# Seven half-products for each pair of second-layer blocks, layer norms by chunk, stepped keys and values, another order of the last blocks

## The chip, the core and the metric

The kernel runs on one core of one Trainium2 chip. The metric is device time in microseconds, the median over runs: 1499.7 us for the kernel before (three runs, 1498.29 to 1500.64). In the text PE is the matrix engine, DVE the vector engine, ACT the scalar engine, POOL the GpSimd engine, and SP the engine from whose queue most DMAs start.

## What is computed

A backbone of two layers over 1024 latent tokens and 256 context tokens of width 1024. Each layer is

```python
h = modulate(rms_norm(x), shift, scale)          # context tokens: a learned constant conditioning
p = h @ w_in                                     # one projection, columns split in head groups
# A: 2-D neighbourhood attention (4 heads of 64, window 8 x 16, plus all context keys)
# B: latent attention: rank-256 queries, rank-128 keys and values, 2-D rotary key
# C: gelu(u) * (layer_norm(v) mixed over 128-token chunks by a 128x128 matrix, 4 groups of 64)
# D: gated depthwise convolution, 3 taps over the tokens
y = concat(A, B, C, D) * silu(gates)
x = x + gate * (y @ w_out)
```

and the output is an RMS norm of the latent tokens. The second layer's context tokens feed nothing after their keys and values.

## The kernel before

Values that enter a matmul are held as two rounded parts, hi and lo, whose sum is the fp32 value. A product of two such values is three matmuls per 128-row slice of the contraction: hi times hi, hi times lo, lo times hi (the helper at L159; transposes go through L162). The normalised input H lies in SBUF with features on the partitions and is cut in token chunks: 0 and 1 of 512 latent tokens each, 2 of 256 context tokens.

`layer(l)` runs in stages. Group C's `cu` and `cv` come first: `cv_tokens` makes the 256 columns of v for 128 tokens at a time, takes mean and variance in 4 groups and normalises the tile (DVE, with a power on POOL in `rstd_of`, L204 to L209, between), and `cv_gate` mixes the normalised tokens by small matmuls. Then `proj` runs over blocks of 128 output columns: cg, dc, dh, db, dg, the value tiles of A (`wav`, 10 tiles of 128 tokens by 288 columns), ckv, cq, ak, aq, bg and ag, two blocks of each but ckv. One block is a 512 KB weight DMA, a cast to hi on ACT (L346), a subtraction for lo on POOL (L351), and for every chunk 24 matmuls (8 slices of the contraction, 3 each) of 512 columns into one PSUM bank, which ACT, DVE or POOL reads off.

Latent attention runs in 8 units of 256 queries (`Mla`). `mla_load` fetches the stored parts, `mla_keys` makes one head pair's keys (evacuated by L770 and L771), `mla_values` all values (L788). Neighbourhood attention follows in 16 units (`Na`); `scores_to` lets the score matmuls run ahead of the rest. `merged` multiplies the heads' results by the gates and splits them (L1134, L1135). `out_block(fb)` then makes 128 columns of the output projection and adds the residual, and `finish` normalises a chunk for the next layer or for the output. In both layers chunk 0's out blocks are put between the last attention units, and the blocks for the other chunks follow after the attention.

SBUF space is a set of tags with so many buffers each (g 24, x 20, wh, wl, wr and st 2 each), and PSUM has 5 banks of the large kind (`psb`). The order of the instructions on each engine is set by a scheduler from the order of the code, data and buffers, except between `pe.chain(True)` and `pe.chain(False)`, where PE keeps the written order. All engines run their queues in order.

## Time and profile before

| | |
|---|---|
| median of 3 runs | 1499.7 us (1498.29 to 1500.64) |
| profiled execution | 1495.95 us, span of its instructions 1494.2 us |
| mean granted clock of PE | 0.992 |
| PE busy | 1422.2 us, 95% of the span |
| weight loads of PE | 1195.2 us, 80% (beside the matmuls) |
| DVE busy | 765.6 us, 51% |
| ACT busy | 573.8 us, 38% |
| POOL busy | 459.2 us, 31% |
| chain that ended last | PE 80%, issue 5%, DVE 5%, POOL 5%, ACT 3%, DMA 1% |

The busy times are sums over the whole span. The chain is the work that ended last, followed back to what released each step, so its shares say which engine would have to be faster for an earlier end. The second layer starts at about 839 us with the first `cu` matmul, its attention at about 1153 us, and the blocks after the attention at about 1426 us.

### The profile page before, as it was taken

Reading aid. Unit: us, or ns where it says so; the run is one execution under the profiler, and the core shown is the slowest. Engines: PE = TensorE matmul, PEld = TensorE weight load, DVE = VectorE, ACT = ScalarE, POOL = GpSimd, SP = SyncE. Lnnn points to the kernel's source line nnn. Section 1 sums busy time; section 2 is a strip of 40 time slices with the busy share of each in tenths; the row PEclk is TensorE's granted clock in tenths of the full one; section 3 lists DMA queues with packets and bytes.
Section 4 is the critical chain, followed back from the end, with each engine's and each line's share of the span. In section 5 each row is a group of like instructions: output and inputs, shape, how many; then the busy total and the mean of one; then the engine's idle time right before and its main releaser. Section 6 shows DMA issues by size and latency. Waiting matters only on the chain.

```text
span 1494.2 us, 23065 instructions
## 1 busy us (share of the span) xinstructions
PE 1422.2 (95%) x8964; PEld 1195.2 (80%) x8964; DVE 765.6 (51%) x1873; ACT 573.8 (38%) x1303; POOL 459.2 (31%) x369
## 2 busy tenths in 40 slices
PE   4999999999998999999999999999999899989987
PEld 2788888988886777678878978898888777778877
DVE  5968657063027666664464752201212677755474
ACT  5611111122227565563342421112223666655542
POOL 2145343041230001536522253412332000155741
PEclk9999999999999999999999999999999999999999
DMA  9513324355451004946333101123465012375331
GB/s 354 191 46 113 106 94 171 103 184 179 142 118 24 1 22 116 166 124 174 124 117 127 37 28 44 46 78 127 163 221 115 0 36 43 104 179 156 100 127 57
DMA packets 80943, 166.46 MB, mean 111 GB/s; under 512 B 8129, under 2 KB 34753, under 8 KB 80705
## 3 DMA queue, kind: packets, MB, share of 16 engines
q1 hardware_dynamic: 63808, 136.66, 27.6%
q0 software_dynamic: 15936, 27.27, 9.0%
q8 instruction: 70, 1.15, 0.3%
q10 hardware_dynamic: 1088, 1.05, 0.2%
q14 instruction: 41, 0.33, 0.1%
HBM read 135.33 MB, written 33.82 MB: 113 GB/s over the span
## 4 chain that ended last, share of the span: by engine, by line
PE 80%; issue 5%; DVE 5%; POOL 5%; ACT 3%; DMA 1%; DVEq 0%; SPq 0%; POOLq 0%; ACTq 0%
PE psb L159 65%; PE pst L162 7%; PE psv L159 7%; PE pst L159 1%; POOL g L1135 1%; POOL s L204 1%; POOL wh L348 1%; POOL wl L351 1%; DVE s L206 1%; DVE s L835 1%; DVE g L494 1%; ACT g L982 1%; ACT pt L731 1%; DMA wr<-in_wtb 1%; DVE pt L729 0%
## 5 line engine op out<-in xcount | busy, mean ns | idle before, releaser
L159 PE MATMUL psb<-g,wh 128*128 128x512 f32 (+1 forms) x2400 | 686.9, 372 | 2.6 <-ACT g L1134 1.5
L159 PEld LDWEIGHTS psb<-g,wh 128*128 128x128 f32 x2400 | 431.7, 189 | 88.1 <-issue 2.0
L159 PE MATMUL psb<-g,wl 128*128 128x512 f32 (+1 forms) x1200 | 443.5, 370 | 2.0 <-DVE wl L351 1.2
L159 PEld LDWEIGHTS psb<-g,wl 128*128 128x128 f32 x1200 | 226.2, 189 | 44.4 <-DVE wl L351 1.6
L351 POOL TENSOR_TENSOR wl<-wr,wh 128x1024 fp32r<-128x1024 f32 (+2 forms) x64 | 150.2, 2348 | 304.9 <-ACT wh L346 297.6
L159 PE MATMUL psb<-g,st 128*128 128x512 f32 (+1 forms) x616 | 160.5, 380 | 11.7 <-DVE g L771 2.9
L835 DVE TENSOR_REDUCE s<-psb 128x1 f32<-128x512 f32 (+1 forms) x200 | 117.1, 589 | 87.7 <-PE psb L159 85.7
L159 PE MATMUL psb<-g,g 128*128 128x256 f32 (+2 forms) x832 | 135.6, 307 | 5.3 <-ACT g L346 3.1
L159 PEld LDWEIGHTS psb<-g,st 128*128 128x128 f32 x616 | 98.6, 193 | 35.6 <-issue 13.5
L159 PEld LDWEIGHTS psb<-g,g 128*128 128x128 f32 x832 | 112.3, 194 | 11.6 <-ACT g L346 3.3
L346 ACT CAST wh<-wr 128x1024 fp32r<-128x1024 f32 (+2 forms) x56 | 56.0, 1006 | 168.6 <-PE psb L159 139.6
L159 PE MATMUL psv<-pt,g 128*64 128x256 f32 (+1 forms) x1312 | 119.5, 331 | 0.6 <-ACT pt L731 0.5
L731 ACT COPY pt<-pst 128x512 f32<-128x512 f32 x116 | 67.9, 585 | 110.1 <-PE pst L162 108.7
L159 PEld LDWEIGHTS psv<-pt,g 128*64 128x64 f32 x1312 | 79.3, 137 | 32.1 <-issue 7.8
L326 DVE CUSTOM_DVE_ANT_0 tmp<-g,x 128x512 f32<-128x512 f32 x112 | 94.3, 893 | 8.2 <-POOL x L459 7.2
L162 PE MATMUL pst<-ident,g 128*128 128x128 f32 x464 | 81.3, 278 | 13.7 <-ACT g L982 7.5
L729 DVE COPY pt<-pst 128x512 f32<-128x512 f32 x116 | 79.0, 683 | 11.7 <-PE pst L162 10.8
L204 POOL TENSOR_TENSOR s<-s,mhalf 128x4 f32<-128x4 f32 (+3 forms) x35 | 37.1, 1060 | 155.0 <-DVE s L264 64.3
L1165 DVE SCALAR_TENSOR_TENSOR x<-psb,modG,x 128x512 f32<-128x512 f32 (+1 forms) x48 | 29.4, 615 | 100.9 <-PE psb L159 59.2
L162 PEld LDWEIGHTS pst<-ident,g 128*128 128x128 f32 x464 | 55.6, 140 | 30.8 <-ACT g L982 10.3
L348 POOL TENSOR_SCALAR wh<-wr 128x1024 fp32r<-128x1024 f32 x16 | 44.4, 2772 | 106.5 <-PE pst L162 64.9
L159 PE MATMUL psb<-st,g 128*128 128x288 f32 (+1 forms) x456 | 64.3, 289 | 0.0
(187 smaller groups left out, 1850.2 us busy)
## 6 DMA issues: line engine op xcount, KB each, us to landing
g<-in_wmod SPq DMA_DIRECT2D x48, 512.0 KB, 4.4
wr<-in_wtb SPq DMA_DIRECT2D x46, 512.0 KB, 3.5
wr<-in_wout SPq DMA_DIRECT2D x27, 512.0 KB, 3.7
st<-in_nab SPq DMA_DIRECT2D x24, 384.0 KB, 3.7
x<-in_xT SPq DMA_DIRECT2D x32, 256.0 KB, 5.6
g<-scr_q POOLq DMA_DIRECT2D x32, 256.0 KB, 7.0
x<-x SPq DMA_DIRECT2D x24, 256.0 KB, 2.4
g<-scr_k POOLq DMA_DIRECT2D x20, 256.0 KB, 5.4
```

Of the source, the lines that this page charges most:

```text
L159: return self._next(nc.tensor.matmul(*p, **k))
L162: return self._next(nc.tensor.transpose(*p, **k))
L204: pool.tensor_tensor(r0, v, mhalf[:, :n], ALU.pow)
L206: dve.scalar_tensor_tensor(t, v, -0.5, r0, ALU.mult, ALU.mult)
L326: dve.tensor_tensor_reduce(junk, w[:, hf * 512:hf * 512 + 512], crow[cond, hf], 1.0, 0.0, ALU.mult, ALU.add, part[:, i, cond, hf:hf + 1])
L346: act.copy(hi, raw)
L348: pool.tensor_scalar(hi, raw, 1.0, None, ALU.mult)
L351: (pool if lo_eng == "pool" else dve).tensor_tensor(lo, raw, f(hi), ALU.subtract)
L729: dve.tensor_copy(dst, src)
L731: act.copy(dst, src)
L835: dve.reduce_max(st["mx"][:, i:i + 1], s_, AX.X)
L1165: dve.scalar_tensor_tensor(xa, p, mod[l]["G"][:, fb, cond:cond + 1], xa, ALU.mult, ALU.add)
```

## The change

In the second layer, blocks 0 and 1 of a kind and chunks 0 and 1 form a two by two product, whose contraction is cut in halves as well. `proj2` computes it by 7 half-products (Winograd's form of Strassen's method), each of 12 matmuls of 512 columns, in place of 4 blocks-by-chunks of 24. Half-products are of sums of weight quarters and sums of quarters of H; two banks keep accumulating over several half-products, and their values in between are copied off (`m1`, `u2`, `z5`). The sums of H are made once, in `right_parts` and `right_sums`, and the sums of weights for every pair, with their own hi and lo. What only context tokens need (ak for chunk 2), ckv and the value tiles come first, in the written order of `paired`. 

In both layers the layer norm of group C takes one power for a chunk and two wide DVE operations, keys are allocated and their DMAs issued ahead (`keys_alloc`), values are made in five steps between the scores, and the second head pair's keys one chunk at a time among the pieces of unit 1. The last out blocks run in the order 7, 0 to 6; block 7 takes the weights that chunk 0's block 7 left, and the norm of chunk 0 ends later. Some of the buffers are in pools that share memory by phase.

```diff
         def cv_tokens(c):
             nt = CHUNKS[c][1] // 128
             vns[c] = T("g", [nt, 4, 64])
+            mv = T("s", [nt, 4, 2])
             for i in range(nt):
                 t = c * 4 + i
                 p = PS("b", [256])
                 mm3(p, [(htok(t, kc, 0), htok(t, kc, 1), wcv(kc, 0), wcv(kc, 1)) for kc in range(KC)])
-                gv = T("v1", [4, 64])
-                act.activation(gv, p.rearrange("p (g n) -> p g n", g=4), AF.Gelu)
+                act.activation(vns[c][:, i], p.rearrange("p (g n) -> p g n", g=4), AF.Gelu)
                 st6 = T("s", [4, 6])
-                mv = T("s", [4, 2])
                 for g in range(4):
-                    dve.bn_stats(st6[:, g, :], gv[:, g, :])
+                    dve.bn_stats(st6[:, g, :], vns[c][:, i, g, :])
                 for g in range(4):
-                    dve.bn_aggr(mv[:, g, :], st6[:, g, :])
-                ve = T("s", [4])
-                dve.tensor_scalar(ve, mv[:, :, 1], EPS, None, ALU.add)
-                r = rstd_of(ve, 4)
-                for g in range(4):
-                    dve.tensor_scalar(vns[c][:, i, g, :], gv[:, g, :], mv[:, g, 0:1], r[:, g:g + 1],
-                                      ALU.subtract, ALU.mult)
+                    dve.bn_aggr(mv[:, i, g, :], st6[:, g, :])
+            ve = T("s", [nt, 4])
+            dve.tensor_scalar(ve, mv[:, :, :, 1], EPS, None, ALU.add)
+            r = rstd_of(ve.rearrange("p t g -> p (t g)"), nt * 4)
+            vn = vns[c].rearrange("p t g n -> p (t g) n")
+            mean = mv.rearrange("p t g k -> p (t g) k")[:, :, 0:1]
+            dve.tensor_tensor(vn, vn, mean.to_broadcast([128, nt * 4, 64]), ALU.subtract)
+            dve.tensor_tensor(vn, vn, r.unsqueeze(2).to_broadcast([128, nt * 4, 64]), ALU.mult)
...
+        def w_op(raw, lo_eng="pool"):
+            t = T(("wh", "wl")[nop[0] % 2], [2, 512], F32R)
+            nop[0] += 1
+            split(t[:, 0, :], t[:, 1, :], raw, lo_eng=lo_eng)
+            return t.rearrange("p h (k n) -> p h k n", k=4)
...
+        def right_parts(i):
+            t = {}
+            for k, (c, kc) in enumerate(((0, i), (1, i), (1, i + 4), (0, i + 4))):
+                t[k] = T("x", [512])
+                pool.tensor_tensor(t[k], f(H[c, kc][:, 0, :]), f(H[c, kc][:, 1, :]), ALU.add)
+            R["11", i], R["21", i], R["22", i] = H[0, i], H[0, i + 4], H[1, i + 4]
+            return t
+        def right_sums(i, t):
+            for name, o, p_, q_ in (("1", 0, 1, 0), ("3", 1, 2, 1), ("2", 2, 2, 0), ("4", 3, 3, 2)):
+                after(dve.tensor_tensor(t[o], t[p_], t[q_], ALU.subtract), gated[1])
+                r = R[name, i] = T("o" if i > 1 and name in "34" else "g", [2, 512], F32R)
+                split(r[:, 0, :], r[:, 1, :], t[o], lo_eng="dve" if name in "12" else "pool")
+        def product(p, w, name, first=True):
+            n = 0
+            for i in range(4):
+                r = R[name, i]
+                for wl_, rl_ in ((0, 0), (0, 1), (1, 0)):
+                    pe.matmul(p, w[:, wl_, i, :], r[:, rl_, :], start=first and n == 0, stop=n == 11,
+                              skip_group_check=True)
+                    n += 1
+        def proj2(base, evac, mid=None):
+            r = {}
+            for j in range(2):
+                for k in range(2):
+                    r[j, k] = T("x", [512])
+                    sp.dma_start(r[j, k], a["wtb"][l, BLOCKS.index(f"{base}{j}")][:, k * 512:(k + 1) * 512])
+            q = T("wr", [2, 512])
+            a11, a12 = w_op(r[0, 0]), w_op(r[0, 1])
+            dve.tensor_tensor(q[:, 1, :], r[0, 0], r[1, 0], ALU.subtract)
+            dve.tensor_tensor(r[1, 0], r[1, 0], r[1, 1], ALU.add)
+            dve.tensor_tensor(q[:, 0, :], r[1, 0], r[0, 0], ALU.subtract)
+            dve.tensor_tensor(r[0, 1], r[0, 1], q[:, 0, :], ALU.subtract)
+            s2, s1 = w_op(q[:, 0, :], "dve"), w_op(r[1, 0])
+            x_, y_ = PS("b", [512]), PS("b", [512])
+            product(x_, a11, "11")
+            m1 = T("tmp", [512])
+            act.copy(m1, x_)
+            product(y_, a12, "21")
+            dve.tensor_tensor(m1, y_, m1, ALU.add)
+            evac(0, m1, 0)
+            s3 = w_op(q[:, 1, :], "dve")
+            product(x_, s2, "2", False)
+            u2 = T("tmp", [512])
+            act.copy(u2, x_)
+            s4 = w_op(r[0, 1], "dve")
+            z_ = PS("b", [512])
+            product(z_, s1, "1")
+            z5 = T("tmp", [512])
+            dve.tensor_copy(z5, z_)
+            if mid is not None:
+                mid()
+            a22 = w_op(r[1, 1])
+            product(x_, s3, "3", False)
+            dve.tensor_tensor(z5, x_, z5, ALU.add)
+            evac(1, z5, 1)
+            product(z_, s4, "22", False)
+            dve.tensor_tensor(u2, z_, u2, ALU.add)
+            evac(1, u2, 0)
+            product(x_, a22, "4", False)
+            evac(0, x_, 1)
...
+        def paired():
+            wav = w_tok(a["wav"][l], 288, ("o", "o"), ("o", "o"))
+            block_c("ak0", 2, lambda c, p: k_evac(c, p, 0))
...
+            w = w_block(a["wtb"][l, BLOCKS.index("ckv0")])
+            ckv_block(2, *w)
+            ckv_block(1, *w)
+            ckv_block(0, *w)
+            cv_gate(0)
+            parts = [right_parts(0)]
+            block_c("ak1", 2, lambda c, p: k_evac(c, p, 1))
+            for fns in late[1:]:
+                fns.pop(0)()
+            av_tile(8, wav)
+            late[-1].pop()()
+            parts.append(right_parts(1))
+            for t in (9, 4):
+                av_tile(t, wav)
+            cv_gate(1)
+            for i in range(2):
+                right_sums(i, parts[i])
+            for t in (5, 6, 7):
+                av_tile(t, wav)
+            for i in range(2, 4):
+                right_sums(i, right_parts(i))
+            for t in range(4):
+                av_tile(t, wav)
+            pe.chain(False)
+            av_windows()
+            proj2("cg", lambda c, p, j: gate(c, p, 4 + j))
...
+            proj2("dc", lambda c, p, j: act.copy(map_(6 + j, c), p))
+            proj2("dh", conv_in)
...
+            proj2("db", mulb)
+            proj2("dg", lambda c, p, j: gate(c, p, 6 + j))
+            proj2("cq", cq_evac)
+            proj2("ak", k_evac)
+            proj2("aq", lambda c, p, j: q_evac(c, p, j, 0.125))
+            cq_stats()
+            proj2("bg", lambda c, p, j: act.activation(map_(2 + j, c), p, AF.Silu))
...
+        def keys_alloc(pair):
+
             K = Ks[pair] = {}
             kctx = T("g", [2, 2, 256], F32R)
+            for c in (2, 0, 1):
+                o, n = CHUNKS[c]
+                for h in range(2):
+                    t = K[h, c] = T("g", [2, n], F32R) if c < 2 else kctx[:, h]
+                    pool.dma_start(t[64:128], scr["kr"][:, :, o:o + n].rearrange("h p n -> p h n"))
...
+                evac(vts[c][:, i:i + 2, :], p, "DA"[c == 1 and i == 0])
+            return [lambda c=c, i=i: step(c, i) for c in range(3) for i in range(0, CHUNKS[c][1] // 128, 2)]
...
+                (dve if c == 1 and fc < 2 else pool).tensor_tensor(t[:, 1, :], m, f(t[:, 0, :]), ALU.subtract)
+        tail = (7, 0, 1, 2, 3, 4, 5, 6)
...
+            proj2("ag", lambda c, p, j: act.activation(map_(j, c), p, AF.Silu), lambda: (mla_load(), mla_keys(0), units[0].prep()))
+            ph.close()
...
+            if u == 1:
+                for n, c in enumerate((2, 0, 1)):
+                    ps_.insert(3 * n + 2, lambda c=c: mla_keys(1, (c,)))
+                ps_.insert(0, lambda: keys_alloc(1))
...
-        scores_to(4)
-        mla_values()
-        scores_to(7)
-        mla_keys(1)
+        for k, fn in enumerate(mla_values()):
+            scores_to(3 + 2 * k)
+            fn()
...
             ks2 = [(1, 0, 512), (2, 0, 256)]
-            for fb in range(8):
-                out_block(fb, ks2, lo_eng="dve")
+            for fb in tail:
+                out_block(fb, ks2, kept[7] if fb == 7 else None, lo_eng="dve")
+                if fb == 7:
+                    rest = stats_sums(accs[k0], 512)
                 if fb == 0:
-                    finish(k0)
+                    finish(k0, rest)
...
             pe.chain(True)
             for i in range(2):
                 k = (1, 256 * i, 256)
-                for fb in range(8):
-                    if i == 0:
+                done = k0 if i == 0 else (1, 0, 256)
+                for fb in tail:
+                    if i == 0 and fb < 7:
                         split(*ws[fb], raws[fb], lo_eng="dve" if fb % 2 == 0 else "pool")
-                    out_block(fb, [k], [t.rearrange("p (k n) -> p k n", k=8) for t in ws[fb]])
-                    done = k0 if i == 0 else (1, 0, 256)
-                    if fb == 0:
+                    out_block(fb, [k], kept[7] if fb == 7 else [t.rearrange("p (k n) -> p k n", k=8) for t in ws[fb]])
+                    if fb == 7:
                         rest = stats_sums(accs[done], done[2], more.get(done))
-                    if fb == 2:
+                    if fb == 1:
                         finish(done, rest)
```

The order of PE's instructions changes as follows in three places. First the start of cg in the second layer; before, with the first chunk's first block (`psb_8893`) and the second chunk's (`psb_8921`), where `wh` and `wl` are the block's hi and lo:

```order
L159 MATMUL psb_8893<-g_7677,wh_8889 128x512 x2
L159 MATMUL psb_8893<-g_7677,wl_8890 128x512
L159 MATMUL psb_8893<-g_7682,wh_8889 128x512 x2
L159 MATMUL psb_8893<-g_7712,wh_8889 128x512 x2
L159 MATMUL psb_8893<-g_7712,wl_8890 128x512
L159 MATMUL psb_8921<-g_8237,wh_8889 128x512 x2
L159 MATMUL psb_8921<-g_8237,wl_8890 128x512
```

and now, one row of each of the products called 11 and 21 (`psb_9381`, `psb_9382`), then the whole products called 1 (`psb_9433`) and 2 (again `psb_9381`), and the first rows of product 3:

```order
L173 MATMUL psb_9381<-g_7639,wh_9365 128x512 x3
L173 MATMUL psb_9382<-g_7659,wl_9368 128x512 x3
L173 MATMUL psb_9433<-g_9070,wl_9378 128x512 x3
L173 MATMUL psb_9433<-g_9086,wl_9378 128x512 x3
L173 MATMUL psb_9433<-g_9197,wl_9378 128x512 x3
L173 MATMUL psb_9433<-g_9221,wl_9378 128x512
L173 MATMUL psb_9381<-g_9078,wh_9375 128x512 x3
L173 MATMUL psb_9381<-g_9094,wh_9375 128x512 x3
L173 MATMUL psb_9381<-g_9205,wh_9375 128x512 x3
L173 MATMUL psb_9381<-g_9229,wh_9375 128x512 x3
L173 MATMUL psb_9433<-g_9221,wl_9378 128x512 x2
L173 MATMUL psb_9381<-g_9074,wh_9413 128x512 x3
```

A bank is taken up again by a later product after its value has been copied off; the scheduler has put ten of the twelve matmuls of product 1 ahead of product 2, and two behind it.

Second the start of the second layer's latent attention; before, the keys of the first head pair (`psb_10731` and the two after it) among the blocks of ag:

```order
L159 MATMUL psb_10676<-g_7712,wh_10639 128x512 x2
L159 MATMUL psb_10676<-g_7712,wl_10640 128x512
L159 MATMUL psb_10703<-g_7677,wh_10645 128x512 x2
L159 MATMUL psb_10731<-g_10662,g_10659 128x256 x3
L159 MATMUL psb_10741<-g_10664,g_10659 128x512 x3
L159 MATMUL psb_10753<-g_10666,g_10659 128x512 x2
L159 MATMUL psb_10703<-g_7677,wl_10646 128x512
```

and now, inside the pair of ag: the end of product 1 (`psb_10751`), the keys (`psb_10855`, `psb_10863`, `psb_10871`), then products 3 and 22:

```order
L173 MATMUL psb_10751<-g_9094,wl_10745 128x512 x3
L173 MATMUL psb_10751<-g_9205,wl_10745 128x512 x3
L173 MATMUL psb_10751<-g_9229,wl_10745 128x512 x3
L173 MATMUL psb_10855<-g_10830,g_10827 128x256 x3
L173 MATMUL psb_10863<-g_10832,g_10827 128x512 x3
L173 MATMUL psb_10871<-g_10834,g_10827 128x512 x3
L173 MATMUL psb_10751<-g_9074,wl_10782 128x512 x3
L173 MATMUL psb_10751<-g_9090,wl_10782 128x512 x3
L173 MATMUL psb_10751<-o_9201,wl_10782 128x512 x3
L173 MATMUL psb_10751<-o_9225,wl_10782 128x512 x3
L173 MATMUL psb_10802<-g_8150,wh_10799 128x512 x3
```

The keys stand whole between two half-products, so PE takes them up at that point or waits there.

Third the blocks after the second layer's attention; before, the last transposes of the attention (`pst_13945`) and the first block (`psb_14012`), whose weights are split just then (`g_13977`, `g_13978`):

```order
L159 MATMUL psv_13772<-pt_13879,g_12159 64x128 x2
L162 MATMUL pst_13945<-ident_66,tmp_13885 128x128 x4
L159 MATMUL psb_14012<-g_13953,g_13977 128x256 x2
L159 MATMUL psb_14012<-g_13953,g_13978 128x256
L159 MATMUL psb_14012<-g_13956,g_13977 128x256 x2
L159 MATMUL psb_14012<-g_13956,g_13978 128x256
```

and now, the last transposes (`pst_14056`), block 7 (`psb_14118`) with kept weights, the sums for the norm (`pst_14148`) and block 0 (`psb_14164`):

```order
L176 MATMUL pst_14056<-ident_66,tmp_13996 128x128 x4
L173 MATMUL psb_14118<-g_14065,wl_14001 128x256
L173 MATMUL psb_14118<-g_14068,wh_14000 128x256 x2
L173 MATMUL psb_14118<-g_14068,wl_14001 128x256
L173 MATMUL psb_14118<-g_14083,wh_14000 128x256 x2
L173 MATMUL psb_14118<-g_14083,wl_14001 128x256
L173 MATMUL psb_14118<-g_14086,wh_14000 128x256 x2
L173 MATMUL psb_14118<-g_14086,wl_14001 128x256
L173 MATMUL pst_14148<-ones_71,tmp_13379 128x2 x4
L173 MATMUL psb_14164<-g_14065,g_14089 128x256 x2
L173 MATMUL psb_14164<-g_14065,g_14090 128x256
```

`g_14065` to `g_14086` are the merged heads. Of block 7's matmuls only the last three read the one that is merged last, and the weights split at that time (`g_14089`, `g_14090`) are wanted one block later.

## Rows read from the trace of the kernel before

**Rows 1.** Stretches: length, busy (x) of PE, PEld, DVE, ACT, POOL, granted clock, DMA.

```profile
440.00:480.00 40.00, 34.76 (x197) 28.15 (x196) 22.75 (x56) 25.62 (x62) 3.55 (x6) 1.00 0.23 37
...
690.00:752.00 62.00, 57.64 (x379) 48.18 (x378) 28.59 (x56) 25.05 (x67) 34.01 (x20) 0.99 0.38 123
...
900.00:1130.00 230.00, 230.00 (x1157) 194.56 (x1156) 39.22 (x70) 47.05 (x75) 71.83 (x52) 1.00 0.35 117
...
1130.00:1180.00 50.00, 44.92 (x220) 37.13 (x218) 22.86 (x47) 24.03 (x55) 8.12 (x13) 0.93 0.31 53
...
1380.00:1445.00 65.00, 58.20 (x402) 50.31 (x400) 37.52 (x61) 32.92 (x71) 43.83 (x21) 0.95 0.30 98
```

**Rows 2.** Timeline of PE in the projections: start, duration, operation.

```profile
885.65 0.63 PE L159 MATMUL psb<-g,wh 128*128 128x512 f32 x2
...
917.15 0.63 PE L159 MATMUL psb<-g,wh 128*128 128x512 f32 x2
```

**Rows 3.** Groups by line and shape in 890 to 1150 us: busy, mean ns, idle.

```profile
L351 POOL TENSOR_TENSOR wl<-wr,wh 128x1024 fp32r<-128x1024 f32 x16 | 38.4, 2400 | 110.6 <-ACT wh L346 110.6
...
L459 POOL TENSOR_TENSOR x<-x,tmp 128x512 f32<-128x512 f32 x5 | 6.4, 1290 | 5.8 <-ACT tmp L457 5.8
...
L366 DVE SCALAR_TENSOR_TENSOR wl<-wr,wh 128x1024 fp32r<-128x1024 f32 x2 | 2.5, 1226 | 2.7 <-ACT wh L365 2.6
...
L539 DVE TENSOR_TENSOR g<-psb,x 128x512 f32<-128x512 f32 x4 | 2.8, 690 | 53.1 <-PE psb L159 53.1
...
L548 DVE SCALAR_TENSOR_TENSOR x<-g,vecs,x 128x512 f32<-128x512 f32 x2 | 5.8, 2882 | 2.9 <-POOL x L546 2.9
...
L550 DVE SCALAR_TENSOR_TENSOR x<-g,vecs,x 128x512 f32<-128x512 f32 x2 | 1.5, 752 | 0.1
```

**Rows 4.** Timelines of DVE and POOL where both work.

```profile
916.17 2.88 DVE L548 SCALAR_TENSOR_TENSOR x<-g,vecs,x 128x512 f32<-128x512 f32 x1 [1.47 <-POOL x L546]
...
916.10 2.40 POOL L351 TENSOR_TENSOR wl<-wr,wh 128x1024 fp32r<-128x1024 f32 x1
...
1433.96 3.39 DVE L351 TENSOR_TENSOR g<-wh,g 128x1024 fp32r<-128x1024 f32 x1
...
1432.91 3.36 POOL L351 TENSOR_TENSOR g<-wr,g 128x1024 fp32r<-128x1024 f32 x1
```

**Rows 5.** Timelines of PE and DVE at the gate of group C, layer 0.

```profile
103.50 3.14 DVE L494 TENSOR_SCALAR g<-v,s,s 128x64 f32<-128x64 f32 x4
...
106.69 0.43 PE L159 MATMUL psb<-tmp,g 128*64 128x128 f32 x2 [1.96 <-DVE g L494]
```

**Rows 6.** Timeline of PE at the start of latent attention, layer 1.

```profile
1168.18 1.59 PE L159 MATMUL psb<-g,st 128*128 128x256 f32 x6 [2.04 <-issue]
...
1171.45 4.82 PE L159 MATMUL psb<-g,st 128*128 128x512 f32 x12 [1.69 <-DVE g L771]
```

**Rows 7.** Timeline of PE in the last out blocks of each layer.

```profile
748.79 0.50 PE L159 MATMUL psb<-g,wh 128*128 128x512 f32 x1 [1.50 <-ACT g L1134]
...
750.94 1.09 PE L162 MATMUL pst<-ident,s 128*128 128x128 f32 x4 [1.65 <-DVE s L209]
...
1429.29 0.66 PE L159 MATMUL psb<-g,g 128*128 128x256 f32 x2 [3.10 <-ACT g L346]
...
1444.80 0.62 PE L162 MATMUL pst<-ident,s 128*128 128x128 f32 x4 [2.04 <-DVE s L209]
```

**Rows 8.** Ten-microsecond stretches behind those idle times.

```profile
750.00:760.00 10.00, 9.06 (x41) 7.79 (x42) 2.26 (x4) 1.82 (x5) 5.61 (x9) 0.83 0.50 157
...
1170.00:1180.00 10.00, 8.13 (x32) 6.77 (x32) 6.77 (x16) 6.57 (x20) 0.00 (x0) 0.66 0.00 0
...
1430.00:1440.00 10.00, 9.23 (x57) 9.24 (x58) 9.55 (x6) 6.78 (x9) 9.74 (x4) 0.69 0.34 107
```

**Rows 9.** DMA issues in 1085 to 1182 us: KB each, median us to landing.

```profile
g<-scr_cq POOLq DMA_DIRECT2D x4, 512.0 KB, 12.1
...
g<-scr_ck POOLq DMA_DIRECT2D x2, 512.0 KB, 8.3
```

323 lines of the change are left out of this document (197 added, 126 removed).

## Prediction

> **What bounds the kernel now.** I read the stretches first. From 900 to 1130 us, where the second layer's projections and value tiles run, PE is busy for all 230 us at full clock, while DVE, ACT and POOL together are busy for 158 [rows 1]. So time there goes with the number of matmul columns. The profiled span lacks PE in five other places, which I read next: 440 to 480 us, where the first layer's latent attention starts (5.24 us idle); 690 to 752, its last blocks (4.36); 1130 to 1180, the start of latent attention in the second layer (5.08); 1380 to 1445, its last blocks (6.80) [rows 1]; and 1.96 at one gate of group C [rows 5]. PE's timeline shows what ends the large ones: keys of latent attention on DVE and an issue [rows 6], merged heads and weights on ACT, and the norm's power chain ending on DVE [rows 7]. Behind three of them a ten-microsecond stretch has a granted clock of 0.83, 0.66 and 0.69, while PE is busy for 9.06, 8.13 and 9.23 us in it [rows 8]; at full clock that work would take 1.54, 2.76 and 2.86 us less.
>
> **Part 1, columns.** A pair of blocks over two chunks took 4 times 24 matmuls of 512 columns and takes 7 times 12: 12 fewer. Ten pairs: 120 fewer. From 885.65 to 917.15 us the timeline goes through 45 groups of three such matmuls in 31.5 us, 0.2333 us each [rows 2]. 120 times 0.2333 is 28.0 us, in a stretch where nothing but PE counts. Term: -28.0. A pair will take 84 times 0.2333, that is 19.6 us.
>
> **Part 2, what the pairs add beside PE.** Per pair: seven weight operands, each a hi on ACT and a lo, of 1024 columns' worth in 512-wide halves; four lo on POOL at 1.29 and three on DVE; four weight sums on DVE; four reads or adds from PSUM on DVE, and two copies on ACT. A POOL operation with 512 columns takes 1.29 us [rows 3]; a DVE operation on 1024 columns from SBUF took 1.23 [rows 3], half of it is 0.61; a DVE read of 512 columns from PSUM 0.69 [rows 3]. DVE: 7 times 0.61 and 4 times 0.69 is 7.0 us, POOL 5.2, and where a gate is multiplied in on POOL (cg, dg) another 5.2. Against 19.6 us of PE all of it is hidden if it comes in time. The buffers let a weight operand be made three products ahead (8.4 us), so I cost it at nothing; without that cover one lo costs 0.6 to 1.3 us of PE, seven times ten of them 43 to 90 us, which is the slower rival below.
>
> Where a bank is taken up again, its value must be copied off first: three places in a pair. Usually another whole product of 2.8 us stands between; in cg and dh the scheduler has left two matmuls, 0.47 us, against a copy of about 0.69 [rows 3] and the way from engine to engine. Bounds: 0 (all covered) to 30 times 0.69, 21 us (none covered). I take the end it is nearer to, some 0.15 us in each pair (an estimate, 0.69 less 0.47 and half of it for the other pairs): +1.5.
>
> **Part 3, the start of the first pair.** Product 1 of cg reads sums of H. From the second gate of group C to it PE has seven value tiles of 24 matmuls with 288 columns (0.131 us each by columns, 22.0 us) and two products (5.6): 27.6 us. In that time DVE makes some 15 differences and 8 lo and 4 weight sums, 27 times 0.61 or 16.5 us, and POOL some 8 sums, 6 lo and 2 weight lo, 16 times 1.29 or 20.6 us. Do the two run beside each other? A DVE operation that read two arrays from SBUF took 0.75 us twice and 2.88 us twice [rows 3]; one of the slow ones began 0.07 us after a POOL operation of 2.40 us and ended with 0.5 us of its own behind it, and in the tail DVE's took 3.39 and POOL's 3.36 in place of 1.23 and 2.40 [rows 4]. So they took turns. The Trainium skill says so as a rule (SBUF — State Buffer, section SBUF: two separate sides): a vector operation with two SBUF inputs and a GpSimd operation that reads SBUF hold the shared port in turn, each for its whole instruction; rows 4 agree, and by the rule taken strictly this place would cost 9.5 us and the sum below would be 6.5 us higher. From the rows alone the bounds are 0 (side by side, 20.6 of 27.6) and 16.5 + 20.6 - 27.6 = 9.5 us (always in turn, nothing begun earlier). POOL's sums need only H and free buffers and can begin ahead of the gate, so I take a third: +3.
>
> **Part 4, the start of latent attention.** In the last pair the keys stand behind four products, 11.2 us after its start, and their loads wait for buffers of H, the first free after product 11 at 2.8 us. The issues of that kind landed 8.3 us after issue, the queries' 12.1 [rows 9]. 2.8 + 8.3 is 11.1: on time by a hair; queries freed behind 8.4 us land at 20.5 where the first use is at about 16. Behind these POOL issues in its queue stands the lo of the next weight operand. Bounds 0 to 4.5 us, taken +2. On the other side, values come in five steps between scores, read off mostly by DVE instead of all by ACT, and the second pair's keys no longer stand in a block in front of PE, where an issue (2.04) and a DVE key (1.69) held it [rows 6]. Second layer: 5.08 idle plus 2.76 of clock is 7.8 at stake; the rest of the softmax chain stays; bounds 0 to -7.8, a bit over half: -4. First layer: 5.24 at stake without a fall of the clock; its loads are not changed but for the early key DMAs: bounds +2 (the key wait moves into unit 1) to -5.2, taken -2.
>
> **Part 5, layer norm by chunk.** 24 small operations of a chunk become 4, one power instead of four. The gate that waited 1.96 us did so behind a normalisation of 3.14 us [rows 5]; the work now ends in two operations of 1024 columns (1.23 each), earlier by some small ones and later by not being spread. Bounds +1 to -2, taken -1.5. In the second layer the gates stand far behind the norm: 0.
>
> **Part 6, last blocks.** First layer: 1.50 on the merged heads and 1.65 on the norm [rows 7], and a clock of 0.83 [rows 8]. Block 7 now needs the last merged heads only for its last three matmuls (5 us later), and the norm's chain has a block between: of 4.36 + 1.54 taken -3.5, bounds 0 to -5.9. Second layer: 3.10 for the first block's weights and 2.04 for the norm [rows 7]. With kept weights PE can go on for 21 matmuls of half the columns, 2.5 us; then block 0 wants its split, which comes behind the last merge on ACT at the same time as before: of 3.10 about 0.6 us is left, and about as much again for the lo. The norm has about the same cover as before, two blocks, and its power still queues behind lo splits of up to 3.4 us on POOL [rows 4]. Of 6.80 + 2.86 taken -4.5, bounds 0 to -9.7.
>
> **Sum.** -28.0 - 1.5 - 2 - 4 - 3.5 - 4.5 + 1.5 + 3 + 2 = -37.0 us. The profiled execution took 1495.95 us (span 1494.2 and 1.75 around it), so 1459.0 in its terms; the median of the runs lies 3.75 us above it, so 1462.7, forecast **1463 us**.
>
> **Rivals.**
> - *Only columns pay.* A wait removed at the starts and in the tail is taken over by the next late engine. For it: the waits there end on ACT, DVE and an issue by turns [rows 6, 7], and DVE is busy for 37.5 of 65 us and POOL for 43.8 in the last blocks [rows 1]. Against: the new order puts independent matmuls just there. -28.0 + 6.5 is -21.5: 1478 us.
> - *The two joints cost their upper bounds.* Start of cg 9.5 and latent start 4.5, and each with a fall of the clock as at 1170 us (2.8): -28 - 15.5 + 1.5 + 14 + 5.6 is -22.4: 1477 us. For it: the turns of rows 4; against: part of POOL's work can start early.
> - *All idle goes.* Of the 30.6 us at stake nothing stays and nothing new comes: -58.6: 1441 us; for it only that each wait has an answer in the change; half-way is 1452.
> - *The weight operands set the pace of the pairs* (slower). Its place is the stretch of ten pairs: DVE's 7 two-array operations stretched as in the tail (3.39 for 1.23, factor 2.8) take 12 us, with 2.8 for PSUM reads, 2.8 for results and 5 to 7 us of waiting for ACT and POOL in a chain: 24.5 instead of 19.6. It decides from 3.8 us per pair; at 4.9 it gives -38.5 + 49 = +10.5: 1510 us. Against it: POOL's share of a pair is 5 to 10 us, and it can block no longer than it works.
> - *No change in time*, if half-products wait as much as they save (2.8 us per pair and no other gain): 1497 to 1503.
>
> **Chances.** Forecast 0.48, only columns 0.18, joints 0.14, all idle 0.09, no change 0.04, pace of the operands 0.07. The forecast, the two cases near 1478 and the half-way of the fourth lie in 1447 to 1488; around a tenth is left below (all idle, fully) and a tenth above. Within 0.2% a measurement of this kernel cannot tell a change: faster 0.89, the same 0.04, slower 0.07.
>
> **What will show it.** Matmuls of 512 columns still 0.233 us apart in the pairs and PE busy by about 28 us less there: part 1. A wait of PE ahead of cg's product 1 or 2, released by DVE or POOL: part 3, right at 3, wrong at 0 or over 6. A wait ahead of the keys or queries in the last pair, released by a DMA: part 4. A clock under 0.9 behind it: the joints. No wait over 2 us and a clock over 0.9 at the last blocks of both layers: part 6; a wait of 3 us there again would make it wrong. Waits spread over every pair, on DVE, ACT or POOL, of more than 1 us per pair would make part 2 wrong and the time over 1480.

## The result and the profile after

The changed kernel takes 1477.47 us (median; 1475.18 to 1478.62) against 1498.99 for the kernel before in the same series: a ratio of 0.986, interval 0.9834 to 0.9886, so 21.5 us less. The forecast was 1463, some 37 us less. Direction and range were right; where the time came from was not. The profiled execution took 1475.18 us with a span of 1473.4, 20.8 less than before.

First the sum over the whole span, as the page of the changed kernel gives it (busy us, share, instructions):

```profile
PE 1392.8 (95%) x8844; PEld 1170.5 (79%) x8844; DVE 860.6 (58%) x1906; ACT 612.8 (42%) x1387; POOL 499.3 (34%) x403
```

PE is busy for 29.4 us less than the 1422.2 of before, so it idles for 80.6 us instead of 72.0. The columns were saved, and part of the saving was lost in new waits. To see where, one lists PE's waits in both timelines, stage by stage. A hand-over is a place where a PSUM bank is copied off before the next product may use it:

| stage | idle of PE before, us | after | what the prediction took (idle and clock) |
|---|---|---|---|
| gate of group C, layer 0 | 2.18 | 2.76 | -1.5 |
| latent attention starts, layer 0 | 6.38 | 4.41 | -2 |
| last out blocks, layer 0 | 4.36 | 0 | -3.5 |
| start of layer 1, ahead of the pairs | 0.46 | 10.11 (1.44 and 8.67) | norm 0; "start of cg": +3 |
| inside the pairs: first lo of cg | 0 | 1.50 | in the same +3 |
| inside the pairs: hand-overs of a bank | 0 | 1.52 | +1.5 |
| inside the pairs: weight operands | 0 | 4.42 | 0 |
| loads for latent attention in ag | 0 | 3.79 | +2 |
| latent attention starts, layer 1 | 5.04 | 3.79 | -4 |
| last out blocks, layer 1 | 6.80 | 1.70 | -4.5 |

The ten rows add up to 8.8 us more idle time; with 29.4 us less busy time that makes 20.6 of the span's 20.8. The stretches of the changed kernel that answer to those of [rows 1] (length, busy us and instructions of PE, PEld, DVE, ACT and POOL, then PE's granted clock, DMA share, GB/s):

```profile
690.00:750.00 60.00, 60.00 (x401) 50.96 (x399) 29.00 (x58) 24.18 (x63) 35.79 (x23) 1.00 0.40 128
...
836.00:870.00 34.00, 24.15 (x167) 22.89 (x168) 18.30 (x77) 7.41 (x16) 29.23 (x19) 0.90 0.11 38
...
933.00:1127.00 194.00, 186.29 (x800) 148.29 (x800) 110.76 (x150) 75.66 (x132) 79.67 (x75) 0.99 0.33 106
...
1127.00:1180.00 53.00, 46.51 (x268) 36.91 (x270) 34.70 (x73) 29.90 (x70) 7.06 (x10) 0.97 0.51 93
...
1365.00:1432.00 67.00, 65.30 (x481) 57.69 (x480) 41.70 (x68) 33.57 (x73) 41.76 (x20) 1.00 0.32 103
```

The last blocks are now full in the first layer and nearly full in the second, at clock 1.00 where [rows 8] had 0.83 and 0.69. The projections, full before, now lack 7.7 us in the pairs and about 10 before them. PE's timeline names the waits (start, duration, operation; in brackets the idle time just before and what ended it):

```profile
105.08 3.36 PE L173 MATMUL psb<-tmp,g 128*64 128x128 f32 x32 [2.76 <-DVE s L500]
...
837.18 0.73 PE L173 MATMUL psb<-g,wh 128*128 128x512 f32 x2 [1.44 <-ACT x L485]
...
866.19 0.58 PE L173 MATMUL psb<-g,wl 128*128 128x256 f32 x1 [8.67 <-POOL wl L365]
...
933.64 2.59 PE L173 MATMUL psb<-g,wh 128*128 128x512 f32 x10 [1.50 <-DVE wh L365]
937.78 1.66 PE L173 MATMUL psb<-g,wh 128*128 128x512 f32 x6 [1.08 <-ACT tmp L730]
967.14 0.73 PE L173 MATMUL psb<-g,wh 128*128 128x512 f32 x2 [1.19 <-ACT wh L360]
980.11 1.67 PE L173 MATMUL psb<-g,wh 128*128 128x512 f32 x6 [0.44 <-ACT tmp L730]
990.76 0.73 PE L173 MATMUL psb<-g,wl 128*128 128x512 f32 x2 [2.04 <-ACT wl L360]
...
1037.93 2.96 PE L173 MATMUL psb<-g,wl 128*128 128x512 f32 x12
1040.73 2.49 PE L173 MATMUL psb<-g,wh 128*128 128x512 f32 x10
...
1113.18 0.72 PE L173 MATMUL psb<-g,wl 128*128 128x512 f32 x2 [1.19 <-ACT wl L360]
1127.54 0.94 PE L173 MATMUL psb<-g,g 128*128 128x512 f32 x3 [1.41 <-DMA g<-scr_ck]
1135.84 0.60 PE L173 MATMUL psb<-g,wr 128*128 128x256 f32 x3 [1.75 <-DMA g<-scr_cq]
...
1414.79 0.39 PE L173 MATMUL psb<-g,wh 128*128 128x256 f32 x1 [0.34 <-DVE g L1346]
1423.40 0.62 PE L176 MATMUL pst<-ident,s 128*128 128x128 f32 x4 [1.36 <-DVE s L223]
```

Twelve matmuls from 1037.93 to 1040.73 are 2.80 us, 0.2333 each as in [rows 2]. The largest wait, 8.67 us, stands at the first use of ckv's weights, and POOL's lo ends it. POOL's own timeline there says why:

```profile
843.16 3.81 POOL L218 TENSOR_TENSOR s<-s,mhalf 128x16 f32<-128x16 f32 x1 [4.07 <-DVE s L504]
846.94 16.90 POOL L687 TENSOR_TENSOR x<-g 128x512 f32<-128x512 f32 x12
863.80 2.34 POOL L365 TENSOR_TENSOR wl<-wr,wh 128x1024 fp32r<-128x1024 f32 x1
```

Twelve sums of H (L687, made in `right_parts`) fill POOL for 16.9 us. The lo behind them, of the block that PE needs first, had its hi from ACT at 843.9:

```profile
842.87 1.05 ACT L360 CAST wh<-wr 128x1024 fp32r<-128x1024 f32 x1 [3.86 <-issue]
```

The scheduler put the sums, which no matmul needs before the pairs begin at about 923, in front of a lo that PE needed at 857.5 (866.19 less 8.67). The releaser named for the 8.67 us (a lo of weights) is not the cause; the cause stands in front of it in its queue.

### The profile page after: what moved, and what is told of

It is laid out like the page before. It is cut to its first block, busy times and chain, and to the rows that moved or that the text cites. A ratio compares the mean times of both kernels' runs of the same rounds, so it can differ in the third digit from the quotient of the medians.

```text
span 1473.4 us, 23094 instructions
## 1 busy us (share of the span) xinstructions
PE 1392.8 (95%) x8844; PEld 1170.5 (79%) x8844; DVE 860.6 (58%) x1906; ACT 612.8 (42%) x1387; POOL 499.3 (34%) x403
## 5 line engine op out<-in xcount | busy, mean ns | idle before, releaser
L173 PE MATMUL psb<-g,wh 128*128 128x512 f32 (+1 forms) x2152 | 582.1, 367 | 7.1 <-ACT tmp L730 1.5
L173 PEld LDWEIGHTS psb<-g,wh 128*128 128x128 f32 x2152 | 384.2, 189 | 81.8 <-ACT tmp L730 2.4
L173 PE MATMUL psb<-g,wl 128*128 128x512 f32 (+1 forms) x1256 | 414.8, 372 | 12.2 <-POOL wl L365 8.7
L173 PEld LDWEIGHTS psb<-g,wl 128*128 128x128 f32 x1256 | 237.7, 190 | 57.0 <-POOL wl L365 10.0
L365 POOL TENSOR_TENSOR wl<-wr,wh 128x1024 fp32r<-128x1024 f32 (+2 forms) x46 | 109.9, 2391 | 192.3 <-ACT wh L360 191.2
L173 PE MATMUL psb<-g,g 128*128 128x256 f32 (+1 forms) x784 | 129.1, 305 | 3.8 <-DMA g<-scr_ck 1.4
L173 PEld LDWEIGHTS psb<-g,g 128*128 128x128 f32 x784 | 105.2, 191 | 10.9 <-issue 2.9
L360 ACT CAST wh<-wr 128x1024 fp32r<-128x1024 f32 (+2 forms) x47 | 43.2, 924 | 99.7 <-PE psb L173 70.2
L218 POOL TENSOR_TENSOR s<-s,mhalf 128x4 f32<-128x4 f32 (+4 forms) x22 | 35.1, 1595 | 80.9 <-DVE s L278 39.5
L1063 ACT ACTIVATE g<-psb,s,rq 128x512 f32<-128x512 f32 x64 | 49.2, 774 | 20.4 <-DVE s L1058 20.3
```

Of the source, the lines that this page charges most:

```text
L173: return self._next(nc.tensor.matmul(*p, **k))
L218: pool.tensor_tensor(r0, v, mhalf[:, :n], ALU.pow)
L360: act.copy(hi, raw)
L365: (pool if lo_eng == "pool" else dve).tensor_tensor(lo, raw, f(hi), ALU.subtract)
L1063: act.activation(dst, sps[i], AF.Exp, bias=nb[:, 1:2], scale=rq[:, 0, tq:tq + 1], accum_out=self.rs[:, t, h, i:i + 1])
```

## The experiments

Each kernel is the changed kernel with the edit shown, or one of the kernels here with a further one; of a longer edit the lines that carry it are shown. The ratio, with its interval, is to the kernel before, which ran on the same chip; between two kernels the ratios are compared. The changed kernel's own is 0.986 [0.9834, 0.9886].

**Pairs undone.** The second layer's projections as standard blocks, the rest as changed.

```diff
-            ph = Phase("prj", ("o",))
-            paired()
+        standard()
+        ag_weights()
```

> The changed kernel with the pairs taken back: the second layer's blocks run as in the kernel before, with 96 matmuls where a pair has 84; norms by chunk, stepped keys and values and the order of the last blocks stay. Theory: the pairs save 28.0 us of columns and cost the waits that the trace shows, 8.67 at ckv, 7.4 in the pairs, 3.8 in ag, less what the old order waits there, so 6 to 9 us more than the changed kernel: 1484 to 1487 us. Rival, columns saved in full and the loss is in the other parts: 20 us more or over, 1497 us or more.

1478.81 us, 0.9882 [0.9864, 0.99]. By the ratios the seven half-products gain some 3 us here, by the profiled executions 6, and the intervals overlap; I had expected 6 to 9. Its profile has PE busy for 1418.0 us and idle for 61.6; the changed kernel 1392.8 and 80.6. So the pairs take 25 us off PE, and 19 of them come back as idle time: 8.67, 1.50, 1.52, 4.42 and 3.79 in the table are 19.9, and the kernel without pairs has one wait of 1.00 in their place.

**The old order of the last blocks.** In both layers blocks 0 to 7 in order, the norm's end where it was, no kept weights, and every lo of the merged heads on POOL.

```diff
-tail = (7, 0, 1, 2, 3, 4, 5, 6)
+tail = tuple(range(8))
```

> The changed kernel with the last blocks' order taken back in both layers (0 to 7, no kept weights, norm as before, the merged lo all on POOL). Theory: the tails were worth their idle time, 4.36 less 0 in the first layer and 6.80 less 1.70 in the second, and 3 to 4 us of clock, less 1.44 waited anew at the second layer's start: 10 to 13 us more than the changed kernel, 1487 to 1490 us. Rival, the end is set by the output's chain and the blocks' weights anyway: 5 us more or less than that.

1493.75 us, 0.9976 [0.9965, 0.9987]. The new order is worth 1.2% or 17 us (12 to 23 by the ends of the two intervals), where I had expected 10 to 13. PE's timeline of this kernel shows the waits of [rows 7] again:

```profile
748.46 0.49 PE L173 MATMUL psb<-g,wh 128*128 128x512 f32 x1 [1.50 <-ACT g L1345]
...
750.60 1.09 PE L176 MATMUL pst<-ident,s 128*128 128x128 f32 x4 [1.65 <-DVE s L223]
...
1425.42 0.80 PE L173 MATMUL psb<-g,g 128*128 128x256 f32 x2 [3.11 <-ACT g L360]
...
1440.92 0.62 PE L176 MATMUL pst<-ident,s 128*128 128x128 f32 x4 [2.12 <-DVE s L223]
```

With three smaller ones these are 11.1 us of idle time against 1.7. Behind them the clock falls (same columns as the stretches above):

```profile
750.00:760.00 10.00, 9.40 (x32) 7.68 (x33) 1.21 (x2) 1.49 (x4) 5.25 (x8) 0.68 0.50 159
...
1420.00:1430.00 10.00, 6.21 (x52) 5.51 (x49) 6.47 (x6) 7.55 (x9) 4.88 (x3) 0.77 0.47 157
1430.00:1440.00 10.00, 8.80 (x66) 8.60 (x64) 9.05 (x6) 2.91 (x5) 10.00 (x4) 0.89 0.19 54
```

Busy time by lost clock is 9.40 x 0.32 + 6.21 x 0.23 + 8.80 x 0.11 = 5.4 us, and with 9.4 of waits 14.8, inside the 12 to 23. In the changed kernel these stretches have clock 1.00.

**The old norm.** `cv_tokens` as before, a power for every tile.

```diff
-            r = rstd_of(ve.rearrange("p t g -> p (t g)"), nt * 4)
+                r = rstd_of(ve, 4)
```

> The changed kernel with the layer norm of group C taken back to one chain for each tile of 128 tokens. Theory: the norm by chunk only moves the wait at the first layer's gate (2.18 us in two waits before, 2.76 in one now): no change, within 1.5 us of the changed kernel. Rival, as predicted, it was worth 1.5 us or more: 1.5 to 3 us slower than the changed kernel.

1491.12 us, 0.9948 [0.993, 0.9966]: 13 us slower. My expectation fell. PE's timeline at the start of layer 1, where the changed kernel waited 1.44 and 8.67:

```profile
862.00 0.58 PE L173 MATMUL psb<-g,wl 128*128 128x256 f32 x1 [3.13 <-POOL wl L365]
...
891.86 0.69 PE L176 MATMUL pst<-ident,s 128*128 128x128 f32 x2 [6.21 <-DVE s L223]
```

With two more, of 1.79 and 4.23, the waits add up to 15.4 us against 10.1, and three ten-microsecond stretches around them have granted clocks of 0.67, 0.66 and 0.66. With PE busy for 4.94, 8.83 and 8.14 us in them the clock takes 7.4 us, against 1.3 in the changed kernel (3.81 us busy at 0.66 from 860 to 870). Together that is 11.4 of the 13 us. POOL's timeline behind the sums:

```profile
871.40 1.02 POOL L218 TENSOR_TENSOR s<-s,mhalf 128x4 f32<-128x4 f32 x1 [2.45 <-DVE s L505]
...
890.52 0.70 POOL L218 TENSOR_TENSOR s<-s,mhalf 128x2 f32<-128x2 f32 x1 [0.80 <-DVE s L577]
```

The tiles' powers (L218 with 4 columns) come one by one from 871 to 889, each after an idle POOL has waited for DVE, and ckv's own power, on which the 6.21 us rest, comes at 890.5; in the changed kernel it stands at 878.25. The next kernel tells whether the norm by chunk is worth anything by itself.

**Pairs undone and the old norm.** Both edits above.

> The changed kernel without the pairs and with the layer norm of group C by tile: of the change only the stepped keys and values, the last blocks' order and the pools are left. Theory, the norm by chunk is worth its 14 us only where the pairs' weights and sums want POOL and DVE at the same time: within 3 us of the run without pairs, 0.987 to 0.990 of the kernel before. Rival, the norm by chunk is worth as much by itself: 8 us or more above the run without pairs, 0.993 or above.

1480.5 us, 0.9876 [0.9856, 0.9895], against 0.9882 with the norm by chunk: nothing. The norm by chunk is worth 13 us with the pairs and none without. Set the other way, pairs with the old norm are about 11 us slower than neither (0.9948 against 0.9876). The wait of 1.44 us at the start of layer 1 comes with the norm by chunk and not with the pairs. PE's timeline of the kernel without pairs has it too:

```profile
841.01 0.73 PE L173 MATMUL psb<-g,wh 128*128 128x512 f32 x2 [1.44 <-ACT x L485]
```

The two kernels with the old norm, and the kernel before, have no wait there.

**Values and keys in blocks.** The two parts of latent attention as they stood before, all values read off by ACT.

```diff
-        for k, fn in enumerate(mla_values()):
-            scores_to(3 + 2 * k)
+        scores_to(4)
+        for fn in mla_values():
             fn()
+        scores_to(7)
+        keys_alloc(1)
+        mla_keys(1)
```

> The changed kernel with the values in one block between the scores, all read off by ACT, and the second pair's keys in one block, as before. Theory, the idle time that the trace shows at the two starts (6.38 and 5.04 us before, 4.41 and 3.79 now): 3 us slower than the changed kernel, and up to 3 more with the clock behind a wait of 2 us. Rival: the softmax chain sets the pace there and the waits only change names: within 1 us of the changed kernel.

1480.72 us, 0.9879 [0.9859, 0.99]; some 3 us slower than the changed kernel, as expected, with overlapping intervals. PE's waits at the two starts are 6.3 and 5.7 us, where the changed kernel has 4.41 and 3.79. A wait like those of [rows 6] is back in PE's timeline:

```profile
1161.04 2.29 PE L173 MATMUL psb<-g,st 128*128 128x256 f32 x9 [2.64 <-issue]
```

**Sums held behind ckv's lo.** Every sum of H waits for the lo of the weights in front of it.

```diff
-                pool.tensor_tensor(t[k], f(H[c, kc][:, 0, :]), f(H[c, kc][:, 1, :]), ALU.add)
+                after(pool.tensor_tensor(t[k], f(H[c, kc][:, 0, :]), f(H[c, kc][:, 1, :]), ALU.add), hold)
```

> The changed kernel with one thing altered: POOL's sums of H are put behind the lo of the ckv weights (those for the last three slices also behind the lo of the second ak block). Theory, order in POOL's queue: twelve sums, 16.9 us, stood ahead of a lo that had been ready; the wait of 8.67 us goes, with about 1 us of half clock behind it: 9 to 10 us less than the changed kernel, about 1468 us. Rival, POOL has too much to do there: the same work only moves, and 4 us or more come back as waits of PE on POOL at the second ak block, at the second gate of group C or at the start of cg: at most 4 us less, 1473 us or more.

1479.94 us, 0.9882 [0.9862, 0.9902]: no gain, where I had expected 9 to 10 us. PE's timeline, and POOL's, of this kernel:

```profile
884.24 0.69 PE L176 MATMUL pst<-ident,s 128*128 128x128 f32 x2 [8.70 <-DVE s L223]
```

```profile
867.09 15.84 POOL L689 TENSOR_TENSOR x<-g 128x512 f32<-128x512 f32 x12
882.90 0.70 POOL L218 TENSOR_TENSOR s<-s,mhalf 128x2 f32<-128x2 f32 x1
```

The wait on the lo is gone, and one of the same length has come: the twelve sums now stand in front of the power of ckv's norm. This shows the queue as the cause (the wait went where the sums went) and that one `after` is not a cure.

**POOL in a written order.** Each POOL operation of the stretch follows the one before it in the code: lo of ckv, four sums, lo of ak1, the first power of ckv's norm, four sums, its other powers, the first gate's multiplications, and the other eight sums around the second gate's.

```diff
+            m = nc.gpsimd.tensor_tensor(*p, **k)
+            if self.on:
+                after(m, self.last)
+                self.last = m
```

> The changed kernel with POOL held to a written order between the first ak block and the second gate of group C: lo of ckv, four sums of H, lo of the second ak block, the power of ckv's norm for chunk 2, four sums, the powers for chunks 1 and 0, the multiplications of the first gate, then the other eight sums. With the sums behind the lo alone the wait of 8.7 us came back in full on the power behind them. Theory, order in POOL's queue: now nothing that PE wants soon stands behind more than four sums (5.6 us), and the wait and its clock go: 7 to 10 us less than the changed kernel, 0.979 to 0.981 of the kernel before. Rival, POOL has not the time: its sums and lo come late at cg instead, and waits of PE on POOL or DVE there grow by 4 us or more: 0.983 or above.

1472.26 us, 0.9821 [0.9801, 0.9841]: some 6 us under the changed kernel, with intervals that overlap a little, where 7 to 10 were expected. The 8.67 us are gone; a wait of 3.08 at 885.96 is left, and this one in front of cg (PE's timeline):

```profile
921.47 4.62 PE L173 MATMUL psb<-g,wh 128*128 128x512 f32 x12 [2.51 <-DVE tmp L570]
```

The copy on DVE that ends it takes 0.18 us; differences (L713) and lo stand in front of it in DVE's queue. The timelines of DVE and then of POOL:

```profile
897.18 7.94 DVE L713 TENSOR_TENSOR x<-x,x 128x512 f32<-128x512 f32 x5
...
909.14 2.48 DVE L713 TENSOR_TENSOR x<-x,x 128x512 f32<-128x512 f32 x4
```

```profile
899.41 6.85 POOL L188 TENSOR_TENSOR x<-g 128x512 f32<-128x512 f32 x4
```

Beside POOL's sums a DVE difference takes 1.59 us, and 0.62 from 909.14 on, where POOL does nothing until 912.52. By the Trainium skill (SBUF — State Buffer, section SBUF: two separate sides) a DVE operation with two SBUF inputs and a POOL operation that reads SBUF keep each other out of a shared port, each until it ends; the two durations agree.

**The same, with the last four sums in POOL's idle time** ahead of the second gate.

```diff
-            cv_gate(1)
             parts.append(right_parts(3))
+            cv_gate(1)
```

> The run with POOL's written order, and only the last four sums of H moved ahead of the second gate's multiplications, into POOL's idle time. Theory, DVE and POOL take turns: the five differences on DVE that took 1.59 us each beside those sums take 0.6 to 0.7 each, and the wait of PE on DVE before cg falls from 2.51 us to under 0.6: 2 to 3 us less than that run, 0.980. Rival, DVE is late by its own work: its differences stay above 1.2 us or the wait stays above 2 us, no change in time.

1468.08 us, 0.9802 [0.9777, 0.9826]. DVE's row is now

```profile
898.51 5.23 DVE L713 TENSOR_TENSOR x<-x,x 128x512 f32<-128x512 f32 x6
```

0.87 us each instead of 1.59, and the wait of 2.51 became 1.28, where less than 0.6 was expected. The time is not told apart from that with the written order alone.

**The next pair's first operands ahead of the last product.** In `proj2` two weight operands of the next pair are made before product 7, and ACT's evacuations stand behind them.

```diff
+            if nxt is not None:
+                w_first(nxt)
             product(x_, a22, "4", False)
```

> The changed kernel with one thing altered: the first two weight operands of each pair are made before the last product of the pair ahead, and ACT's last evacuations (in the pairs cg, dc and bg, and the convolution) come behind them. Theory, order in ACT's queue: the casts stood behind evacuations that wait for the last product; the three waits of PE on ACT at the starts of dh, db and ag (1.19, 2.04 and 1.19 us) go: 3.5 to 4.5 us less, about 1473.5 us. Rival, the operands are late as a whole (loads, lo on POOL): the waits stay under another name, within 1 us of 1477.5.

1474.69 us, 0.985 [0.9832, 0.9868]: not told apart from the changed kernel. Of the three waits on casts the 1.19 at dh went (one of 0.87 on POOL came), and the 1.19 at ag went (one of 0.53 on DVE came). The 2.04 at the start of db went too: PE goes through the pair's first products from 990.43 without a wait. But one as long came 9 us later, inside the pair. The timelines of PE, ACT and DVE:

```profile
1001.54 1.02 PE L173 MATMUL psb<-g,wh 128*128 128x512 f32 x2 [2.08 <-ACT wh L362]
...
1000.35 1.14 ACT L362 CAST wh<-x 128x512 fp32r<-128x512 f32 x2 [2.18 <-DVE x L727]
...
993.11 3.23 DVE L880 SCALAR_TENSOR_TENSOR x<-x,vecs,x 128x511 f32<-128x511 f32 x4
```

The cast waits for a sum of weights that DVE makes at 999.58 (L727), and the convolution's operations (L880) stand between the sums in DVE's queue. The wait on the queries' loads grew from 1.75 to 2.68. Half right. With POOL's written order beside it:

> The order of POOL as in the run beside it, and the first two weight operands of each pair ahead of the last product of the pair before. Theory: both gains add, 1 to 3 us less than with POOL's order alone, 0.977 to 0.980 of the kernel before, the best of all. Rival: an earlier end of the first stretch only moves the waits for the loads in the pair of ag (2.7 and 1.1 us on the queries' load when the operands were early), and nothing is added.

1469.62 us, 0.9806 [0.9784, 0.9827]: some 2 us under the written order alone, within the intervals. In PE's timeline the queries' wait is longer still:

```profile
1131.66 0.59 PE L173 MATMUL psb<-g,wr 128*128 128x256 f32 x3 [3.38 <-DMA g<-scr_cq]
```

What PE gains in the pairs it waits for at the next DMA, so the loads are the next thing to move.

**All of it, and the queries' loads ahead.** Both orders, the last four sums ahead of the second gate, ckv's last norm one value tile later, and the loads of cq issued ahead of those of kr.

```diff
-            keys_alloc(0)
             for c in (0, 1) if last else (2, 0, 1):
...
                     pool.dma_start(cq[c, j], scr["cq"][:, j * 128:(j + 1) * 128, o:o + n].rearrange("h p n -> p h n"))
+            keys_alloc(0)
```

> POOL's order and the early first operands as in the run of both, and three places mended: the last four sums of H ahead of the second gate's multiplications (POOL stood idle there), ckv's last norm one value tile later, and the issues of the queries' loads ahead of the rotary keys' in POOL's queue. Theory: the waits of PE of 3.08 and 2.51 us on DVE before cg and of 3.38 and 1.32 us on the queries' loads go, with some clock: 6 to 10 us less than the run of both, 0.974 to 0.977 of the kernel before. Rival, the transfers themselves are the limit (8.2 MB in 50 us there) and the scores now wait for the rotary keys: at most 4 us less, 0.978 or above.

1462.86 us, 0.9759 [0.974, 0.9779]: faster than both kernels. The stretch from 840 to 900, of this kernel and then of the changed one:

```profile
840.00:900.00 60.00, 60.00 (x457) 56.25 (x456) 43.23 (x109) 12.39 (x26) 44.20 (x28) 1.00 0.14 49
```

```profile
840.00:900.00 60.00, 51.33 (x377) 48.02 (x378) 27.82 (x97) 10.65 (x21) 38.65 (x25) 0.94 0.13 45
```

PE no longer waits there at all, with 80 matmuls more in the same 60 us, and of the waits on loads 0.72 us is left. One large wait stays, again on the small copy behind DVE's differences (PE's timeline):

```profile
922.26 6.93 PE L173 MATMUL psb<-g,wl 128*128 128x512 f32 x22 [4.08 <-DVE tmp L572]
```

**That copy on ACT.**

```diff
-            dve.tensor_copy(KR[:, t, :], p[:, 256:288])
+            (act.copy if last else dve.tensor_copy)(KR[:, t, :], p[:, 256:288])
```

> The run with loads and sums mended, and the 32 rotary columns of the second layer's value tiles copied off by ACT instead of DVE. Theory: product 21 of cg waits 4.08 us for a bank whose last reader is such a copy of 0.18 us, behind some nine differences and lo on DVE; with the copy on ACT that wait goes, and PE waits at product 1 or 2 instead for what DVE still has to make, 1 to 2 us: 2 to 3 us less than that run, 0.974. Rival, DVE's work sets the start of cg: the whole 4 us come back one product later, no change, 0.976.

1463.09 us, 0.9768 [0.9747, 0.979]: no change. The 4.08 became two waits at the hand-overs, this one and one of 1.29 (PE's timeline):

```profile
924.49 4.60 PE L173 MATMUL psb<-g,wh 128*128 128x512 f32 x12 [2.14 <-ACT tmp L751]
```

## Why the prediction was right, and where it was wrong

**Columns (part 1): right.** 0.2333 us each, and 28.0 of the 29.4 us that PE is busy for less.

**Start of the first pair (part 3): the step that failed.** The prediction said that POOL's sums "need only H and free buffers and can begin ahead of the gate", and took that as help. They began ahead of it, twelve of the sixteen in one piece, and in a queue that runs in order they held up the lo of ckv's weights. The wait that I looked for, ahead of cg's first products, is there with 1.50 us; the one that cost stands 67 us earlier, 8.67 us with a clock of 0.90 in its stretch. The joint costs 10.2 us of idle time (8.67 and 1.50), not 3, and more than the 9.5 that I took for the upper bound. The rival "two joints cost their upper bounds" had this size (14 us for both; measured 10.2 here and 3.8 at ag), but not the place. That this wait is a matter of the written order is shown: holding the sums moved it, and an order removed it.

**The pairs' operands (part 2): "at nothing" was wrong by 4.4 us.** Three waits end on a hi cast on ACT that stood behind the work on the last product's results, as at dh, whose weights were issued by 937 and needed 7.8 us to land (ACT's timeline):

```profile
965.98 0.58 ACT L849 COPY x<-psb 128x512 f32<-128x512 f32 x1 [1.01 <-PE psb L173]
966.46 0.62 ACT L360 CAST wh<-x 128x512 fp32r<-128x512 f32 x1
```

The buffers allow three products ahead; ACT's queue allowed none at a change of pair. That is shown: with the first two operands made earlier all three waits went, though others of 0.87, 2.08 and 0.53 us came behind them. The hand-overs, taken at 1.5 us, measured 1.08 and 0.44. The slower rival, operands that set the pace, did not come: from 933 to 1127 PE is busy for 186.3 of 194 us.

**Loads in ag (part 4): right in kind, +3.8 for +2**, and the order of the loads in POOL's queue is the likely lever: with the queries' issues first the wait on loads is 0.72 us, though that kernel has other edits too. Starts of latent attention: in the second layer -1.25 us of idle time and -1.3 of clock (8.35 us busy at 0.83 from 1150 to 1160, against the 0.66 of [rows 8]) for -4, in the first -1.97 for -2; undoing keys and values costs some 3 us.

**Norm by chunk (part 5): the size was wrong.** In the second layer I took 0. It brings the wait of 1.44 us there; in the time it is worth nothing without the pairs and 13 us with them. By the timelines that is because the tiles' powers no longer go back and forth between DVE and POOL while ckv's norm waits behind them; this reason was read and not tested by itself. In the first layer the gates wait 2.76 us where they waited 2.18, 1.96 of it in [rows 5]: a small loss, inside my bounds, where I had taken a small gain.

**Last blocks (part 6): right in kind, half the size.** I took 8 us out of 15.6 at stake; the runs show 17 (12 to 23). Both layers' terms were too small: by idle time and clock the first gave 5.9 us (4.36 and 1.54, all of it) for 3.5, the second 8.0 (5.10 and 2.86) for 4.5. In the second, "of 3.10 about 0.6 us is left, and about as much again for the lo" became 0.34, and a wait of about 2 us for the norm of [rows 7] became 1.36. The clock came back entirely, where I had counted only part of it.

Put together: the rivals "only columns pay" (1478) and "joints" (1477) have the measured number. The mechanism of the first is refuted: the last blocks paid 17 us, keys and values 3, and of the columns' 28 all but some 3 was eaten. The second had the size of what was lost. That the time still lies in my range is in part luck, since errors cancel: the start of the first pair took 7 us more than I had counted, the norm and its gates 3, the operands 4.4 and the loads 1.8, while the last blocks gave 6 to 9 us more. With the queues put in order the same half-products reach 1462.9 us, near my forecast, but by edits that the changed kernel did not have. What stays open is what each of these edits is worth: together they give 14.6 us (1477.5 to 1462.9), but the intervals of one step and the next overlap.

## What to carry to other kernels

When work is moved off the critical path onto an engine with spare time, ask what stands behind it in that engine's queue: a scheduler that fills idle time with work that is ready can put 17 us of it in front of a 2 us operation that is needed now. Read such a wait two steps back, from PE to the releaser, and from the releaser to what its engine was doing while its inputs lay ready. A gain on PE and a gain in the order of the last blocks are separate, so undo each alone before saying which one paid.

## What the runs showed of the hardware that was not expected

Small DVE operations can lose as much to POOL as large ones. In the changed kernel's DVE timeline the operations of one norm, of 16 elements a partition, take 1.2 us each beside POOL's sums, and one of them takes 0.17 us in a pause of POOL (876.39):

```profile
847.01 1.25 DVE L220 SCALAR_TENSOR_TENSOR s<-s,s 128x16 f32<-128x16 f32 x1 [2.79 <-POOL s L218]
848.29 1.22 DVE L221 TENSOR_TENSOR s<-s,s 128x16 f32<-128x16 f32 x1
...
856.63 1.21 DVE L508 TENSOR_TENSOR g<-g,s 128x1024 f32<-128x1024 f32 x1
...
876.39 0.17 DVE L221 TENSOR_TENSOR s<-s,s 128x16 f32<-128x16 f32 x1
```

So these tiny operations cost about 1 us more in a stretch in which POOL works. Not every operation pays: the one of 1024 columns at 856.63 stands beside the same sums and takes 1.21 us, and at 843.00, ahead of them, it takes 1.22. And POOL's power grows with its elements: 3.81 and 2.91 us for 16 a partition in the changed kernel, 1.01 for 4 and 0.70 for 2 in the kernel with the old norm. One power instead of four saves POOL 0.2 to 1.1 us; what it saves beside are the ways between the engines.
